# Conformer convolution: GpSimd's additions become accumulating DMAs into four partial sums, and the tap diagonals come from memory

## The chip, the cores and the metric

The program runs on one core of one Trainium2 chip. The metric is the device time of one execution in microseconds. Before the change it is 2589.65 us, the median of three runs (2588.46 to 2589.95).

## The reference, cut to what matters

The whole program is two transformer blocks of two layers each on a sequence of 512 tokens with 1024 features, in float32. The change lies in one of its mixers, the Conformer convolution of the second block, and in the padding of small tiles elsewhere.

```python
def conformer_conv(h, w_pw1, b_pw1, w_dw, b_dw, ln_g, ln_b, w_pw2, b_pw2):
    a, gt = jnp.split(h @ w_pw1 + b_pw1, 2, axis=-1)
    z = a * jax.nn.sigmoid(gt)
    z = lax.conv_general_dilated(
        z, w_dw[:, None, :], window_strides=(1,), padding=[(CONV_WIDTH - 1, 0)],
        dimension_numbers=('NWC', 'WIO', 'NWC'), feature_group_count=D_MODEL) + b_dw
    z = jax.nn.silu(layernorm(z, ln_g, ln_b))
    return z @ w_pw2 + b_pw2
```

So each of 1024 channels is convolved over time with its own 31 taps: y[t] is the sum over k of w[k] z[t - 30 + k].

## The kernel before, in words

Activations stand with 128 channels on the partitions and 512 tokens along the row; the 1024 channels are eight tiles, 0 to 7. Every matrix product in float32 is made of three TensorE matmuls (`mm3`, L325 to L327) on a high and a low half of each operand. `load` (L315, L307) brings a block of weights with one DMA of 512 KB issued by SyncE (SP) into `raw` (3 buffers), then ScalarE (ACT) casts it to `hi` and VectorE (DVE) subtracts to get `lo` (3 buffers each). In the trace, PE is TensorE, PEld its weight loads, POOL is GpSimd.

The Conformer stage (`conformer`, L1194) runs through the tiles in the order of `CONV_ON` (L193). For each tile the two halves of the first projection are made (`pw1`, two blocks of 24 matmuls), then `evict` (L1329) makes z with DVE and ACT, and `conv` (L1214) hands the tile's 31 taps out. The list says to whom: tiles 0, 2 and 5 wholly to DVE (`by_vector`, one multiply-and-add L1273 per tap, 90 in all beside the first tap, which is ACT's at L1231); tiles 1 and 3 wholly and 19 taps of tile 4 to ACT and POOL together (`by_pool`: ACT multiplies z by the tap, L1285, into `pr`, 4 buffers, and POOL adds `pr` to the sum `zc`, L1289, 79 times); 12 taps of tile 4 and all of tiles 6 and 7 to PE (`by_pe`, L1304: each tap is a product with a diagonal matrix, three matmuls into the bank `pcv`, 74 taps). The diagonals are made on the chip by `build` (L1296): ACT writes the high half `dh` (L1300), DVE the low half `dl` (L1301).

What is done beside what is set by the fillers `bg["v"]`, `bg["g"]`, `bg["p"]`, which hand out steps at a nominal price, and in the end by the scheduler, which lays down one fixed order for each engine. Each engine then works strictly in its order.

When three tiles are ready, `provisional` (L1255) sums them (L1258, L1259), PE makes their mean (`pm`), and every tile is shifted by it (`shift`, L1268), squared and summed (`centre`). After the last tile four columns of sums (`pd`, `pst`) give the layer norm, and the second projection (`pw2`) begins.

Of the kernel before, what the change touches and what calls it, by code (L numbers as in the profile page):

```python
# [2 lines left out]

# [1 line left out]

# [5 lines left out]
F32 = mybir.dt.float32  # L11
# [6 lines left out]
P = 128  # L18
# [41 lines left out]
def _lay_out(i):  # L60
# [98 lines left out]
    o["pw1"] = pairs(g["conv_w_pw1_2"][0], D)  # L159
    o["pw2"] = per_tile(g["conv_w_pw2_2"][0])  # L160

    q = np.arange(P)[:, None]
    c = np.arange(T)[None, :] - 384
    f = np.float32
# [26 lines left out]
PRIO_W = 100  # L191
CONV_V = .55
CONV_ON = [(0, "v", 0), (1, "g", 0), (2, "v", 0), (3, "g", 0), (4, "g", 12), (5, "v", 0), (6, "v", 31), (7, "v", 31)]  # L193
AHEAD = 12
NT_F = 2
NT_N = 2
GRP = 8
X_AT = (0, 1, 2)
ON_N = (1, 3)
ON_NV = (0,)  # L200
# [54 lines left out]
def _body(ctx, tc, a, out):  # L255
# [14 lines left out]

    def narrow(pool, n, dt=F32, **kw):

        return pool.tile([P, -(-n // 16) * 16], dt, **kw)[:, :n]

    nvec = a["vecs"].shape[1]
    vecs = narrow(cp, nvec, name="vecs")
# [221 lines left out]
    class Head:  # L498
# [4 lines left out]

        def scores(self):
            pool = self.pool
            nm = narrow(pool, NQ, name="nm", tag="nm", bufs=3)
            sm = narrow(pool, NQ, name="sm", tag="sm", bufs=3)
            self.p = []
            for i in range(NQ):
                n = P * (i + 1)  # L510
                acc = bank("sc")
                self.score(acc[:, :n], i, n)
                lg = pool.tile([P, n], F32, name=f"lg{i}", tag=f"lg{i}", bufs=2)
                V.tensor_tensor_reduce(out=lg, in0=acc[:, :n], in1=self.mask[:, T - n :], scale=-self.scale,  # L514
                                       scalar=3e38, op0=OP.add, op1=OP.min, accum_out=nm[:, i : i + 1])
                S.activation(lg, lg, AF.Exp, bias=nm[:, i : i + 1], scale=-1.0, accum_out=sm[:, i : i + 1])  # L516
                self.p.append(lg)
            rc = narrow(pool, NQ, name="rc", tag="rc", bufs=3)
            V.reciprocal(rc, sm)  # L519
            if self.rows_scale is not None:  # L520
                V.tensor_mul(rc, rc, self.rows_scale)
            for i in range(NQ):
                if i in self.on_s:
                    S.activation(self.p[i], self.p[i], AF.Copy, scale=rc[:, i : i + 1])
                else:
                    (V if i in self.on_v else G).tensor_scalar(self.p[i], self.p[i], rc[:, i : i + 1], None, op0=OP.mult)  # L526
# [373 lines left out]
    def nsa():  # L900
        with ExitStack() as es:
# [46 lines left out]
            with phase("n_x") as pool:  # L948
# [8 lines left out]
                def c_proj(m):  # L957
                    w = load(a["nsa_c"][m], NC8)
                    acc = bank()
                    yield from lin(acc, w, xs, range(NC8), sl(0))  # L960

                    def out():
                        bl = pool.tile([P, 16, 2, 32], F32, name="bl")
                        for g in range(2):
                            kst = pool.tile([P, T + 16], F32, name="kst", tag="kst")
# [112 lines left out]
            def u_task(gi):  # L1078
# [13 lines left out]
                hd = pool.tile([P, 16], F32, name="hd")  # L1092
# [20 lines left out]
            def cmp_scores(g):  # L1113
# [12 lines left out]
                mx = pool.tile([P, NQ * 4], F32, name="cmx", tag="cmx")  # L1126
# [3 lines left out]
                sm = pool.tile([P, NQ, 4], F32, name="csm", tag="csm")  # L1130
# [63 lines left out]
    def conformer():  # L1194
        with ExitStack() as es:
# [8 lines left out]

            with phase("c_x") as pool:

                nw = 31 * NC8
                wdw = vecs[:, _VECS["w_dw"][0] : _VECS["w_dw"][0] + nw]
                wdh = narrow(pool, nw, F32R, name="wdh")
                wdl = narrow(pool, nw, name="wdl")  # L1210
                S.copy(wdh, wdw)
                V.tensor_sub(wdl, wdw, bc(wdh))

                def conv(j, z, on, n_pe):  # L1214

                    y = zc[:, j]
                    if n_pe:
                        zh = narrow(pool, T + 30, F32R, name="zh", tag="zh", bufs=2)
                        zl = narrow(pool, T + 30, F32R, name="zl", tag="zl", bufs=2)
                        for t in (zh, zl):  # L1220
                            G.memset(bc(t[:, :30]), 0.0)
                        split(zh[:, 30:], zl[:, 30:], z)
                        bg["p"].push(j, by_pe(j, y, zh, zl, n_pe))
                    if n_pe < 31:
                        bg[on].push(j, (by_vector if on == "v" else by_pool)(j, y, z, n_pe))

                def start(j, y, z, n_pe):
                    if n_pe:
# [46 lines left out]
                        yield 660.0  # L1275
                    convolved(j)

                def by_pool(j, y, z, n_pe):
                    taps = list(start(j, y, z, n_pe))
                    prs = []  # L1280
                    for n in range(len(taps) + 3):
                        if n < len(taps):
                            sh = 30 - taps[n]
                            pr = pool.tile([P, T], F32, name="pr", tag="pr", bufs=4)
                            S.activation(pr[:, sh:], z[:, : T - sh], AF.Copy, scale=vec("w_dw", j * 31 + taps[n]))  # L1285
                            prs.append((pr, sh))
                        if n >= 3:
                            pr, sh = prs.pop(0)
                            G.tensor_add(y[:, sh:], y[:, sh:], pr[:, sh:])  # L1289
                        yield 1170.0  # L1290
                    convolved(j)

                taps = iter([j * 31 + k for j in order for k in range(plan[j][1])])
                diags = []

                def build(n):  # L1296
                    for t in islice(taps, n):
                        dh = pool.tile([P, P], F32R, name="dh", tag="dh", bufs=AHEAD + 2)
                        dl = pool.tile([P, P], F32R, name="dl", tag="dl", bufs=AHEAD + 2)
                        S.activation(dh, ident, AF.Copy, scale=vec("w_dw", t))  # L1300
                        V.tensor_scalar(dl, ident, wdl[:, t : t + 1], None, op0=OP.mult)  # L1301
                        diags.append((t, dh, dl))

                def by_pe(j, y, zh, zl, n_pe):  # L1304
                    acc = bank("pcv")
                    for k in range(n_pe):
                        build(1)
                        t, dh, dl = diags.pop(0)
                        assert t == j * 31 + k
                        mm3(acc, dh, dl, zh[:, k : k + T], zl[:, k : k + T], k == 0, k == n_pe - 1)  # L1310
                        yield STEP
                    if n_pe < 31 or not shifted:
                        S.activation(y, acc, AF.Identity, bias=vec("b_dw", j))
# [15 lines left out]
                def evict(j, acc, acg):  # L1329
                    sg = pool.tile([P, T], F32, name="sg", tag="sg", bufs=2)  # L1330
                    V.tensor_mul(sg, acg, norm.b)
                    at_s = S.activation(sg, sg, AF.Sigmoid, bias=vec("b_pw1", 8 + j))
                    z = pool.tile([P, T], F32, name="z", tag="z", bufs=8)
                    V.tensor_mul(z, acc, norm.b)  # L1334
                    at_v = V.scalar_tensor_tensor(z, z, vec("b_pw1", j), sg, op0=OP.add, op1=OP.mult)  # L1335
                    conv(j, z, *plan[j])
                    with tc.issue_after(at_s.ins), tc.issue_after(at_v.ins):
                        build(min(GRP, AHEAD - len(diags)))

                for j in order:  # L1340
                    accs = []
# [103 lines left out]
```

## Time and profile before

| | |
|---|---|
| median of three runs | 2589.65 us |
| the profiled execution, its own time | 2589.92 us |
| its span, first to last instruction | 2588.1 us |
| PE busy | 2512.7 us (97%) |
| DVE busy | 1626.9 us (63%) |
| ACT busy | 1141.1 us (44%) |
| POOL busy | 467.1 us (18%) |
| DMA queues, share of 16 engines' span | 26.6% |

The page cuts the span into 40 slices of 65 us. Read along PE's row of digits there is a 9 almost everywhere, and 7s and 8s in three or four slices from the thirty-first on: that is the Conformer stage. The granted clock of PE dips in the same slices. A stage is best read with the view that gives each engine's busy time by stretch, then the chain of waits in that stretch, then the groups of instructions by line.

### The profile page before, as it was taken

To read this page: it belongs to the slowest core of one execution; us is meant where nothing else is said; L and a number is where in the kernel's file an instruction comes from. 1 tells how busy PE (TensorE), PEld (TensorE's weight loads), DVE (VectorE), ACT (ScalarE), POOL (GpSimd) and SP (SyncE) were. 2 spreads that over 40 slices of the span, in tenths; PEclk is the share of its full clock that TensorE was granted. 3 is DMA by queue.
4 is the path that set the end of the run, shared out by engine and by line. 5 is a ranking of instruction groups with operands and counts; after the bars stand their busy time and mean duration, and the time that the engine had idled before them with its cause. 6 is when DMAs were issued, how large, how long until landed. Compare 5 with 4: busy or idle time off the path is not lost. (4 is left out here: it accounts for less than half of the span.)

```text
span 2588.1 us, 31317 instructions
## 1 busy us (share of the span) xinstructions
PE 2512.7 (97%) x11903; PEld 2088.8 (81%) x11903; DVE 1626.9 (63%) x2495; ACT 1141.1 (44%) x1933; POOL 467.1 (18%) x369
## 2 busy tenths in 40 slices
PE   8999999999999999999999999999999778999998
PEld 6988888888888888888888888888887556888886
DVE  7887777635677657777436996444338996544422
ACT  4664444424566544444334684322225453333221
POOL 3452000001132212000011222000004763100001
PEclk9999999999999999999999999999999878999998
DMA  4121333333211222332333212333332101323332
GB/s 151 59 67 66 106 98 98 92 96 104 90 55 56 72 73 90 99 97 93 93 97 114 65 54 82 98 98 96 90 100 74 57 17 33 99 97 98 94 98 70
DMA packets 65447, 218.90 MB, mean 85 GB/s; under 512 B 7536, under 2 KB 8560, under 8 KB 65296
## 3 DMA queue, kind: packets, MB, share of 16 engines
q1 hardware_dynamic: 65296, 216.90, 26.6%
q8 instruction: 93, 1.52, 0.2%
q14 instruction: 58, 0.48, 0.1%
HBM read 214.70 MB, written 2.10 MB: 84 GB/s over the span
## 5 line engine op out<-in xcount | busy, mean ns | idle before, releaser
L307 ACT CAST hi<-raw 128x1024 fp32r<-128x1024 f32 (+4 forms) x417 | 420.7, 1011 | 905.2 <-PE acc L326 707.0
L327 PE MATMUL acc<-xsh,lo 128*128 128x512 f32 x1792 | 701.1, 392 | 14.1 <-DVE lo L307 14.1
L325 PE MATMUL acc<-xsh,hi 128*128 128x512 f32 x1792 | 700.8, 392 | 3.0 <-ACT xsh L307 2.9
L326 PE MATMUL acc<-xsl,hi 128*128 128x512 f32 x1792 | 701.0, 391 | 1.0 <-DVE xsl L309 1.0
L307 DVE TENSOR_TENSOR lo<-raw,hi 128x1024 fp32r<-128x1024 f32 (+4 forms) x417 | 499.8, 1199 | 314.4 <-ACT hi L307 309.1
L327 PEld LDWEIGHTS acc<-xsh,lo 128*128 128x128 f32 x1792 | 338.7, 189 | 87.7 <-DVE lo L307 17.0
L325 PEld LDWEIGHTS acc<-xsh,hi 128*128 128x128 f32 x1792 | 338.8, 189 | 73.6 <-ACT xsh L307 3.3
L326 PEld LDWEIGHTS acc<-xsl,hi 128*128 128x128 f32 x1792 | 338.6, 189 | 73.2 <-DVE xsl L309 2.3
L377 POOL TENSOR_TENSOR ssum<-ssum,sq 128x512 f32<-128x512 f32 x75 | 120.8, 1614 | 1471.5 <-ACT sq L371 1461.4
L325 PE MATMUL acc<-hh,hi 128*128 128x512 f32 x704 | 277.4, 394 | 0.0
L327 PE MATMUL acc<-hh,lo 128*128 128x512 f32 x704 | 276.0, 392 | 0.0
L326 PE MATMUL acc<-hl,hi 128*128 128x512 f32 x704 | 273.2, 388 | 0.0
L526 POOL TENSOR_SCALAR lg<-lg,rc 128x384 f32<-128x384 f32 (+3 forms) x144 | 166.9, 1176 | 378.9 <-DVE rc L519 303.9
L714 DVE TENSOR_TENSOR y<-acc,r 128x512 f32<-128x512 f32 x88 | 60.5, 691 | 219.7 <-PE acc L327 219.5
L461 DVE TENSOR_TENSOR x<-x,acc 128x512 f32<-128x512 f32 x104 | 70.5, 684 | 153.5 <-PE acc L327 153.0
L327 PEld LDWEIGHTS acc<-hh,lo 128*128 128x128 f32 x704 | 132.1, 188 | 31.0
L326 PEld LDWEIGHTS acc<-hl,hi 128*128 128x128 f32 x704 | 132.2, 188 | 29.6
L325 PEld LDWEIGHTS acc<-hh,hi 128*128 128x128 f32 x704 | 132.3, 188 | 26.3
L1289 POOL TENSOR_TENSOR zc<-zc,pr 128x496 f32<-128x496 f32 (+17 forms) x79 | 127.7, 1620 | 64.5 <-ACT pr L1285 56.0
L711 DVE SCALAR_TENSOR_TENSOR y<-u,vecs,y 128x510 f32<-128x510 f32 (+1 forms) x176 | 130.9, 748 | 3.4 <-ACT y L709 0.6
L516 ACT ACTIVATE lg<-lg,nm 128x128 f32<-128x128 f32 x192 | 107.1, 560 | 47.4 <-DVE nm L514 46.4
L307 ACT CAST hh<-y 128x512 fp32r<-128x512 f32 x88 | 54.7, 621 | 135.5 <-DVE y L718 135.5
(366 smaller groups left out, 3841.4 us busy)
## 6 DMA issues: line engine op xcount, KB each, us to landing
raw<-in_ffn_in SPq DMA_DIRECT2D x88, 512.0 KB
raw<-in_swi_in SPq DMA_DIRECT2D x88, 512.0 KB
raw<-in_ffn_out SPq DMA_DIRECT2D x32, 448.0 KB
raw<-in_swi_out SPq DMA_DIRECT2D x32, 448.0 KB
raw<-in_pw SPq DMA_DIRECT2D x24, 512.0 KB
raw<-in_fox_qk SPq DMA_DIRECT2D x16, 512.0 KB
raw<-in_ffn_out SPq DMA_DIRECT2D x16, 512.0 KB
raw<-in_uqk SPq DMA_DIRECT2D x16, 512.0 KB
```

What stands on the lines that cost most here:

```text
L307: return S.copy(hi, src), V.tensor_sub(lo, src, bc(hi))
L325: PE.matmul(acc, lh, rh, start=first, stop=False)
L326: PE.matmul(acc, lh, rl, start=False, stop=False)
L327: last_mm[0] = PE.matmul(acc, ll, rh, start=False, stop=last).ins
L377: (sum_on or G).tensor_add(self.s, self.s, sq)
L461: V.tensor_add(x[:, c], x[:, c], acc)
L516: S.activation(lg, lg, AF.Exp, bias=nm[:, i : i + 1], scale=-1.0, accum_out=sm[:, i : i + 1])
L526: (V if i in self.on_v else G).tensor_scalar(self.p[i], self.p[i], rc[:, i : i + 1], None, op0=OP.mult)
L711: V.scalar_tensor_tensor(y[:, sh:], u[:, : T - sh], vec(f"cw{l}{2 - sh}", jj), y[:, sh:], op0=OP.mult, op1=OP.add)
L714: V.tensor_mul(y, acc, norm.b)
L1289: G.tensor_add(y[:, sh:], y[:, sh:], pr[:, sh:])
```

## The change

GpSimd's addition is replaced by a DMA that it issues and that accumulates (`accum_op=OP.add`): the DMA engines read `pr`, add it to the destination and write it. The sum of a tile is spread over four partial sums (`CHAINS = 4`): the sum `zc` itself and three tiles `part`, whose first taps ACT writes directly. After the last tap two DMAs add two of the partial sums to the other two, and a third joins those. So 70 DMAs carry products and 9 join partial sums, 79 in all, each of up to 128 x 2 KB (256 KB). `pr` has 8 buffers.

The diagonals are laid out beforehand on the host (`dwd`, 8 taps in a block of 128 x 1024) and come through `load`: 10 blocks, seven of 8 taps, two of 7 and one of 4. `build`, `wdh` and `wdl` go. Narrow tiles are padded to 128 bytes instead of 64, and three small tiles of a softmax head become slices of one.

```diff
+    wd = g["conv_w_dw_2"][0]
+    dg = np.zeros((sum(-(-n // 8) for _, _, n in CONV_ON), P, 8, P), np.float32)
...
+            dg[b + k // 8, np.arange(P), k % 8, np.arange(P)] = wd[k, j * P : (j + 1) * P]
...
+    o["dwd"] = dg.reshape(-1, P, RAW)
...
-AHEAD = 12
+CHAINS = 4
+STEP_G = 1000.0
...
-        return pool.tile([P, -(-n // 16) * 16], dt, **kw)[:, :n]
+        return pool.tile([P, -(-n // 32) * 32], dt, **kw)[:, :n]
...
-            nm = narrow(pool, NQ, name="nm", tag="nm", bufs=3)
-            sm = narrow(pool, NQ, name="sm", tag="sm", bufs=3)
+            small = narrow(pool, 3 * NQ, name="nm", tag="nm", bufs=3)
+            nm, sm, rc = (small[:, NQ * z : NQ * z + NQ] for z in range(3))
...
-                def by_pool(j, y, z, n_pe):
+                def by_dma(j, y, z, n_pe):
+
                     taps = list(start(j, y, z, n_pe))
-                    prs = []
...
-                            pr = pool.tile([P, T], F32, name="pr", tag="pr", bufs=4)
-                            S.activation(pr[:, sh:], z[:, : T - sh], AF.Copy, scale=vec("w_dw", j * 31 + taps[n]))
...
-                            G.tensor_add(y[:, sh:], y[:, sh:], pr[:, sh:])
-                        yield 1170.0
+                    parts = [y]
+                    for n, k in enumerate(reversed(taps)):
+                        sh = 30 - k
+                        if len(parts) < CHAINS:
+                            part = pool.tile([P, T], F32, name="part", tag="part", bufs=2 * (CHAINS - 1))
+                            if sh:
+                                G.memset(part[:, :sh], 0.0)
+                            S.activation(part[:, sh:], z[:, : T - sh], AF.Copy, scale=vec("w_dw", j * 31 + k))
+                            parts.append(part)
+                        else:
+                            pr = pool.tile([P, T], F32, name="pr", tag="pr", bufs=8)
+                            S.activation(pr[:, sh:], z[:, : T - sh], AF.Copy, scale=vec("w_dw", j * 31 + k))
+                            G.dma_start(parts[n % CHAINS][:, sh:], pr[:, sh:], accum_op=OP.add)
+                        yield STEP_G
+                    while len(parts) > 1:
+                        half = len(parts) // 2
+                        for to, of in zip(parts[:half], parts[half:]):
+                            G.dma_start(to, of, accum_op=OP.add)
+                        parts = parts[:half]
+                        yield STEP_G
                     convolved(j)
...
                     for k in range(n_pe):
-                        build(1)
-                        t, dh, dl = diags.pop(0)
-                        assert t == j * 31 + k
-                        mm3(acc, dh, dl, zh[:, k : k + T], zl[:, k : k + T], k == 0, k == n_pe - 1)
+                        if k % 8 == 0:
+                            n = min(8, n_pe - k)
+                            wh, wl = load(a["dwd"][first[j] + k // 8][:, : n * P], n)
+                        mm3(acc, wh[:, k % 8], wl[:, k % 8], zh[:, k : k + T], zl[:, k : k + T], k == 0, k == n_pe - 1)
```

Outside the Conformer stage the order and the waits of every engine stay as they were. Inside it they move at three places. Names in square brackets are what a row waits for: the engines by name, `DMAHW` a load of SP's, and `DMASW0` to `DMASW7` the landing of one of the eight latest DMAs that POOL issued.

On POOL, at the end of tile 1's taps. Before:

```order
L1289 TENSOR_TENSOR zc<-zc,pr 128x508 [waits Activation_49,Pool_49]
L1289 TENSOR_TENSOR zc<-zc,pr 128x509 [waits Activation_49,Pool_49]
L1289 TENSOR_TENSOR zc<-zc,pr 128x482 [waits Activation_49]
L1289 TENSOR_TENSOR zc<-zc,pr 128x510 [waits Activation_49,Pool_49]
L1289 TENSOR_TENSOR zc<-zc,pr 128x483 [waits Activation_49,Pool_49]
L1289 TENSOR_TENSOR zc<-zc,pr 128x511 [waits Activation_49,Pool_49]
```

After:

```order
L1293 DMA zc<-pr 128x507 [waits Activation_49]
L1293 DMA part<-pr 128x506 [waits Activation_49]
L1293 DMA part<-pr 128x505 [waits Activation_49]
L1298 DMA zc<-part 128x512 [waits DMASW7_49,DMASW1_49,Pool_49]
L1293 DMA part<-pr 128x504 [waits DMASW2_49,DMASW0_49,Activation_49]
L1298 DMA part<-part 128x512 [waits DMASW3_49,Pool_49]
L1293 DMA zc<-pr 128x503 [waits DMASW4_49,Activation_49]
L1293 DMA part<-pr 128x502 [waits DMASW5_49,Activation_49]
L1293 DMA part<-pr 128x501 [waits DMASW6_49,Activation_49]
L1293 DMA part<-pr 128x500 [waits DMASW0_49,Activation_49]
L1298 DMA zc<-part 128x512 [waits DMASW7_49,DMASW1_49]
```

Each addition waited for the one before it on POOL itself. Now each DMA waits for the landing of the DMA four places earlier, on the same partial sum, and the joins (L1298) stand in the same queue.

On DVE, where the first two finished tiles are summed. Before:

```order
L1273 SCALAR_TENSOR_TENSOR zc<-z,vecs,zc 128x496 [waits DVE_49]
L1334 TENSOR_TENSOR z<-acc,r 128x512 [waits PE_49]
L1258 TENSOR_TENSOR s_17771<-zc 128x512 [waits DVE_49,Pool_49]
L307 TENSOR_TENSOR lo<-raw,hi 128x1024 [waits DMAHW0_49,Activation_49]
L1273 SCALAR_TENSOR_TENSOR zc<-z,vecs,zc 128x497 [waits DVE_49]
```

After:

```order
L1273 SCALAR_TENSOR_TENSOR zc<-z,vecs,zc 128x499 [waits DVE_49]
L1258 TENSOR_TENSOR s_17517<-zc 128x512 [waits DMASW5_49,DMASW6_49,DMASW1_49,Pool_49]
L1273 SCALAR_TENSOR_TENSOR zc<-z,vecs,zc 128x484 [waits DVE_49]
L1273 SCALAR_TENSOR_TENSOR zc<-z,vecs,zc 128x500 [waits DVE_49]
L1334 TENSOR_TENSOR sg<-acc,r 128x512 [waits PE_49]
L1273 SCALAR_TENSOR_TENSOR zc<-z,vecs,zc 128x485 [waits DVE_49]
L315 TENSOR_TENSOR lo<-raw,hi 128x1024 [waits DMAHW1_49,Activation_49]
```

The sum over tiles 0 and 1 waited for POOL; now DVE's queue waits there for the landing of tile 1's joins, and the `lo` behind it is the first block of diagonals.

On ACT, at the last products of tile 4. Before:

```order
L1285 ACTIVATE pr<-z,vecs 128x501 [waits Pool_49]
L1300 ACTIVATE dh<-ident,vecs 128x128 [waits PE_49] x2
L1285 ACTIVATE pr<-z,vecs 128x502 [waits Pool_49]
L1300 ACTIVATE dh<-ident,vecs 128x128 [waits PE_49] x2
L1313 ACTIVATE zc<-pcv,vecs 128x512 [waits PE_49]
L1285 ACTIVATE pr<-z,vecs 128x503 [waits Pool_49]
```

After:

```order
L315 CAST hi<-raw 128x896 [waits DMAHW6_49,PE_49]
L1292 ACTIVATE pr<-z,vecs 128x497 [waits DMASW7_49,Activation_49]
L1292 ACTIVATE pr<-z,vecs 128x496 [waits DMASW0_49,Activation_49]
L1292 ACTIVATE pr<-z,vecs 128x495 [waits DMASW1_49]
L1292 ACTIVATE pr<-z,vecs 128x494 [waits DMASW2_49,Activation_49]
L315 CAST hi<-raw 128x1024 [waits DMAHW7_49,DVE_49,PE_49]
L315 CAST hi<-raw 128x1024 [waits DMAHW0_49,DVE_49,PE_49]
L315 CAST hi<-raw 128x1024 [waits DMAHW1_49,DVE_49,PE_49]
```

The single diagonals between the products are gone. Each product waits for the landing of the DMA that read its buffer last, and the casts of tile 7's diagonals (the three rows at the end) stand behind the last product of all.

## Rows read from the trace of the kernel before

**Rows 1.** Engines by stretch: busy us (instructions), PE's granted clock, DMA share, GB/s.

```profile
core 0: us, PE busy (x) PEld busy (x) DVE busy (x) ACT busy (x) POOL busy (x), PEclk, DMA share, GB/s
1900.00:1940.00 40.00, 40.00 (x177) 32.81 (x176) 11.84 (x14) 10.94 (x13) 4.38 (x3) 1.00 0.33 101
1980.00:2060.00 80.00, 65.92 (x252) 51.87 (x251) 79.97 (x65) 36.29 (x54) 60.88 (x38) 0.89 0.18 60
2060.00:2140.00 80.00, 57.27 (x182) 39.41 (x181) 79.96 (x108) 46.42 (x105) 55.08 (x38) 0.79 0.06 20
2140.00:2160.00 20.00, 10.81 (x46) 8.31 (x45) 16.07 (x29) 4.48 (x10) 5.58 (x5) 0.79 0.00 0
```

**Rows 2.** Chain of waits from 1957 to 2165 us, shares by engine and line.

```profile
by line: DVE zc L1273 41.6%; DVE dl L1301 17.4%; DVE lo L307 10.7%; issue 7.0%; DVE z L1335 4.4%; DVE zl L307 2.4%; DVE zc L1268 2.0%; DVE z L1334 1.9%; DVE d L1241 1.8%; DVE ssum L377 1.8%; PE acc L325 1.2%; DVE sg L1331 1.1%; PE pd L1365 
```

**Rows 3.** Groups by line, 1957 to 2155 us: busy us, mean ns, idle before, releaser.

```profile
L1289 POOL TENSOR_TENSOR zc<-zc,pr 128x496 f32<-128x496 f32 (+17 forms) x79 | 127.7, 1620 | 64.5 <-ACT pr L1285 56.0 <-DVE lo L307 4.5
L1273 DVE SCALAR_TENSOR_TENSOR zc<-z,vecs,zc 128x482 f32<-128x482 f32 (+21 forms) x90 | 99.4, 1122 | 0.2
L1285 ACT ACTIVATE pr<-z,vecs 128x494 f32<-128x494 f32 (+15 forms) x79 | 52.8, 699 | 1.7 <-POOL zc L1289 1.7
L1301 DVE TENSOR_SCALAR dl<-ident,wdl 128x128 fp32r<-128x128 f32 x74 | 42.1, 607 | 0.0
L327 PE MATMUL pcv<-zh,dl 128*128 128x512 f32 x74 | 35.3, 477 | 14.5 <-DVE dl L1301 14.2
L1300 ACT ACTIVATE dh<-ident,vecs 128x128 fp32r<-128x128 f32 x74 | 26.0, 390 | 8.8 <-PE pcv L326 8.6
L307 DVE TENSOR_TENSOR lo<-raw,hi 128x1024 fp32r<-128x1024 f32 x15 | 24.5, 1632 | 5.2 <-ACT hi L307 5.2
L1335 DVE SCALAR_TENSOR_TENSOR z<-z,vecs,sg 128x512 f32<-128x512 f32 x8 | 11.9, 1490 | 0.2 <-ACT sg L1332 0.2
```

**Rows 4.** Instructions in order of time on DVE and POOL: start us, us.

```profile
1964.76 2.23 DVE L1273 SCALAR_TENSOR_TENSOR zc<-z,vecs,zc 128x484 f32<-128x484 f32 x3
1968.26 1.22 DVE L307 TENSOR_TENSOR lo<-raw,hi 128x1024 fp32r<-128x1024 f32 x1
1972.30 17.19 POOL L1289 TENSOR_TENSOR zc<-zc,pr 128x482 f32<-128x482 f32 x10 [20.02 <-ACT pr L1285]
1982.83 2.26 DVE L307 TENSOR_TENSOR lo<-raw,hi 128x1024 fp32r<-128x1024 f32 x1
1988.30 5.09 DVE L1273 SCALAR_TENSOR_TENSOR zc<-z,vecs,zc 128x496 f32<-128x496 f32 x3
```

**Rows 5.** The stage's marks in order of time: first projection, products, last taps, second projection.

```profile
1943.59 0.40 PE L325 MATMUL acc<-xsh,hi 128*128 128x512 f32 x1
1971.53 2.46 ACT L1285 ACTIVATE pr<-z,vecs 128x482 f32<-128x482 f32 x4
2153.21 0.74 DVE L1317 SCALAR_TENSOR_TENSOR zc<-pcv,vecs,cmean 128x512 f32<-128x512 f32 x1
2154.73 1.87 PE L1365 MATMUL pd<-ones,d 128*128 128x1 f32 x8 [7.32 <-DVE d L1241]
2163.91 1.65 PE L325 MATMUL acc<-xsh,hi 128*128 128x512 f32 x3 [2.94 <-ACT xsh L307]
```

**Rows 6.** DMAs: a load's issue and its first reader, two stretches of full queues.

```profile
1.19 0.42 SPq L284 DMA_DIRECT2D x<-in_xt  x1
4.19 0.69 DVE L373 TENSOR_TENSOR ssum<-x 128x512 f32<-128x512 f32 x1 [4.19 <-DMA x<-in_xt]
...
8.00:10.00 2.00, 0.94 (x2) 0.03 (x1) 1.73 (x2) 1.09 (x2) 1.30 (x2) 1.00 1.04 412
2582.00:2584.00 2.00, 0.00 (x0) 0.00 (x0) 1.16 (x2) 0.00 (x0) 0.03 (x1) 0.50 1.02 382
```

More of the change, by code (lines that the diff above doesn't have):

```diff
@@ L1 @@
 from contextlib import ExitStack
-from itertools import islice
 import numpy as np
@@ L160, in _lay_out @@
     o["pw2"] = per_tile(g["conv_w_pw2_2"][0])
+    wd = g["conv_w_dw_2"][0]
+    dg = np.zeros((sum(-(-n // 8) for _, _, n in CONV_ON), P, 8, P), np.float32)
+    b = 0
+    for j, _, n in CONV_ON:
+        for k in range(n):
+            dg[b + k // 8, np.arange(P), k % 8, np.arange(P)] = wd[k, j * P : (j + 1) * P]
+        b += -(-n // 8)
+    o["dwd"] = dg.reshape(-1, P, RAW)
     q = np.arange(P)[:, None]
@@ L193 @@
 CONV_ON = [(0, "v", 0), (1, "g", 0), (2, "v", 0), (3, "g", 0), (4, "g", 12), (5, "v", 0), (6, "v", 31), (7, "v", 31)]
-AHEAD = 12
+CHAINS = 4
+STEP_G = 1000.0
 NT_F = 2
 NT_N = 2
-GRP = 8
 X_AT = (0, 1, 2)
@@ L517, in scores @@
                 self.p.append(lg)
-            rc = narrow(pool, NQ, name="rc", tag="rc", bufs=3)
             V.reciprocal(rc, sm)
@@ L964, in out @@
                         for g in range(2):
-                            kst = pool.tile([P, T + 16], F32, name="kst", tag="kst")
+                            kst = narrow(pool, T + 16, name="kst", tag="kst")
                             G.memset(kst[:, T - 1 :], 0.0)
@@ L1091, in u_task @@
                 wd = 2 << gi
-                hd = pool.tile([P, 16], F32, name="hd")
+                hd = narrow(pool, 16, name="hd")
                 V.tensor_mul(hd, cur[:, :16], cinv[:, sl(gi, 16)])
@@ L1125, in cmp_scores @@
                                            2.0 ** -(g * 4 + r + 1), a4[:, :, r], op0=OP.mult, op1=OP.add)
-                mx = pool.tile([P, NQ * 4], F32, name="cmx", tag="cmx")
+                mx = narrow(pool, NQ * 4, name="cmx", tag="cmx")
                 V.tensor_reduce(out=mx, in_=lg, axis=AX.X, op=OP.max)
@@ L1129, in cmp_scores @@
                 S.activation(lg, lg, AF.Exp)
-                sm = pool.tile([P, NQ, 4], F32, name="csm", tag="csm")
+                sm = narrow(pool, NQ * 4, name="csm", tag="csm").rearrange("p (i r) -> p i r", r=4)
                 V.tensor_reduce(out=sm.rearrange("p i r -> p (i r)"), in_=lg, axis=AX.X, op=OP.add)
@@ L1205, in conformer @@
             with phase("c_x") as pool:
[L1207 to L1212, printed above, removed]
                 def conv(j, z, on, n_pe):
@@ L1224, in conv @@
                     if n_pe < 31:
-                        bg[on].push(j, (by_vector if on == "v" else by_pool)(j, y, z, n_pe))
+                        bg[on].push(j, (by_vector if on == "v" else by_dma)(j, y, z, n_pe))
                 def start(j, y, z, n_pe):
@@ L1276, in by_vector @@
                     convolved(j)
-                def by_pool(j, y, z, n_pe):
+                def by_dma(j, y, z, n_pe):
                     taps = list(start(j, y, z, n_pe))
-                    prs = []
-                    for n in range(len(taps) + 3):
-                        if n < len(taps):
-                            sh = 30 - taps[n]
-                            pr = pool.tile([P, T], F32, name="pr", tag="pr", bufs=4)
-                            S.activation(pr[:, sh:], z[:, : T - sh], AF.Copy, scale=vec("w_dw", j * 31 + taps[n]))
-                            prs.append((pr, sh))
-                        if n >= 3:
-                            pr, sh = prs.pop(0)
-                            G.tensor_add(y[:, sh:], y[:, sh:], pr[:, sh:])
-                        yield 1170.0
-                    convolved(j)
@@ L1293, in conformer @@
[L1293 to L1302, printed above, removed]
+                    parts = [y]
@@ L1304, in by_pe @@
+                    while len(parts) > 1:
[4 more added lines that the diff above has]
+                        yield STEP_G
+                    convolved(j)
+                first = {}
+                for c, _, n in CONV_ON:
+                    first[c] = sum(-(-m // 8) for d, _, m in CONV_ON if d < c)
                 def by_pe(j, y, zh, zl, n_pe):
@@ L1331, in evict @@
                     V.tensor_mul(sg, acg, norm.b)
-                    at_s = S.activation(sg, sg, AF.Sigmoid, bias=vec("b_pw1", 8 + j))
+                    S.activation(sg, sg, AF.Sigmoid, bias=vec("b_pw1", 8 + j))
                     z = pool.tile([P, T], F32, name="z", tag="z", bufs=8)
                     V.tensor_mul(z, acc, norm.b)
-                    at_v = V.scalar_tensor_tensor(z, z, vec("b_pw1", j), sg, op0=OP.add, op1=OP.mult)
+                    V.scalar_tensor_tensor(z, z, vec("b_pw1", j), sg, op0=OP.add, op1=OP.mult)
                     conv(j, z, *plan[j])
-                    with tc.issue_after(at_s.ins), tc.issue_after(at_v.ins):
-                        build(min(GRP, AHEAD - len(diags)))
                 for j in order:
```

## The prediction

> **What bounds the kernel now.** I read the busy times by stretch first. For 40 us before the Conformer stage PE is busy all of the time at clock 1.00, 177 matmuls, 0.226 us each. Between 1980 and 2140 us DVE is busy 159.9 of 160 us, PE only 123.2, and PE's granted clock averages 0.89 and 0.79 of its 2.4 GHz, that is, part of the stretch at 1.2 GHz; the DMA engines are nearly idle (0.18 and 0.06) [rows 1]. So in this stage, and only here, DVE sets the pace. The chain of waits says the same: of 1957 to 2165 us, 41.6% is DVE's tap L1273 and 17.4% its low diagonals L1301, which PE waits for [rows 2, 3]. The next question is why DVE is so slow. The order of time shows it: three taps take 2.23 us before POOL starts its additions at 1972.30 and 5.09 us while POOL adds; a `lo` takes 1.22 and then 2.26 us [rows 4]. Both engines slow each other down; POOL's own additions take 1.62 us and leave it 64.5 us idle [rows 3].
>
> After the Trainium skill (SBUF — State Buffer, Who interferes with whom) a DVE instruction with two SBUF inputs contends with a GpSimd instruction that reads SBUF, not with one that only writes. The first half agrees with the two prices of a tap, 0.74 and 1.70 us; no row here shows a GpSimd that only writes descriptors.
>
> **The change part by part.** I count on the clock of the profiled execution (span 2588.1, own time 2589.92, 0.3 us above the median). Everything ahead of the stage keeps order and waits; the wider padding and the merged small tiles change no instruction's size, and I price them at nothing. The sum is the time at which the second projection starts, 2163.9 us before [rows 5].
>
> *DVE.* From 1957 to 2155 it is busy about 198 us without a gap. The 74 low diagonals go: -42.1. The 90 taps at 0.72 (mean of the eight ahead of 1972.30, as the 2.23 us for three also show) instead of 99.4 us: -34.6. The eight L1335 at 0.75 instead of 11.9 us: -5.9; three `zl` likewise: -2.9. The `lo` become 25 of 1.22 instead of 15 with 24.5 us: +6.0 [rows 3, 4]. Net -79.5: DVE's own work would end at 2075.5.
>
> *PE.* The first projection starts at 1943.59 [rows 5]; 384 matmuls of it and 222 of taps at 0.226 us are 137.0 us, small matmuls 2.5: it could be done at 2083.1. From the last eviction (2153.21) to the second projection it is 10.7 us [rows 5], work of the layer norm that the change does not touch. So PE's floor is 2093.8, a gain of 70.1 us.
>
> *ACT.* 79 products stay (52.8 us, nine of them written straight into partial sums); 74 high diagonals go (26.0), ten casts of about 1.0 come. ACT gets lighter by 16 us and is under half busy. But each product now waits for a landing, and casts that PE needs are behind products.
>
> *Loads.* Ten more on SP's queue, at most 5.2 MB, in a stretch where the DMA engines are used 0.06 to 0.18 [rows 1]: hidden as prefetch while three buffers are free; they share the engines with the additions, which I count below.
>
> *The additions.* 79 DMAs. The first product for one is ready at about 1974 (three products of the row at 1971.53 fill the partial sums) [rows 5]. Let T be the time from one DMA to the next. Nothing in the trace shows an accumulating DMA, or any issued by POOL, so I bound T. Full queues move 382 to 412 GB/s [rows 6]: 256 KB in 0.64 to 0.69 us. From below: an addition costs as much as a copy, 0.69, and 26 loads of 512 KB at about 1.31 us share the engines with 79 additions, 0.43 each: 1.1. If reading the destination counts as much again: 1.8. A load of 256 KB is read 3.0 us after its issue [rows 6]; if the four partial sums didn't overlap at all, T would be 3.0. I take 1.5, between the two ends that keep the four in flight; the full range is 1.1 to 3.0. POOL's own part in each issue is not shown either; SP's takes 0.42 [rows 6], POOL's old addition 1.62 [rows 3], so it doesn't move these ends.
>
> Three places turn T into a time. (a) Last landing: 1974 + 79 T, plus 12 for joins that nothing overlaps (one landing of 3.0 for each of the first two tiles, two for the last), plus about 11 (shift, square and sum 1.8, then 9.2 from `pd` at 2154.73 to 2163.91 [rows 5]): 1997 + 79 T. (b) The casts of tile 7's diagonals are behind the last product, which needs the landing of about the 66th DMA: 1974 + 66 T + 9, cast and `lo` 2, 93 matmuls 21, layer norm 10.7: 2017 + 66 T. (c) PE's floor, 2094. The latest counts. At T = 1.5 these are 2115.5, 2116 and 2094; the second projection starts at 2116 to 2117, 47 us earlier. On DVE the sum over tiles 0 and 1 (L1258) then waits for about the 39th landing, 1974 + 39 x 1.5 + 9 = 2041, where DVE would be at about 2020; behind it stand z of later tiles and the first block's `lo`. With 58 us of its work left it still ends by 2100, inside (a) and (b).
>
> Forecast: 2589.9 - 47 = 2543, to the median less 0.3: 2542. (What PE's higher clock gives back is in the sum, since the matmuls were priced at 0.226.)
>
> **The rivals.** *The DMAs are hidden* (T up to 1.2): PE's floor decides, 2589.9 - 70 = 2520. For it: 0.69 us of transfer and 1.1 with the loads. Against: three queues with hardly any slack, each waiting for landings.
>
> *An addition reads twice* (T = 1.8). Both operands are read by the DMA engines, so the transfer doubles to 1.38, with loads 1.8: (a) gives 2139, 25 us earlier, 2565. This is still faster. The Trainium skill (Collectives: The Full Stack, The bandwidth ceiling) puts the half rate of its ReduceScatter down to exactly that, two source reads per chunk on one ring; no run here shows it yet.
>
> *The DMA queue becomes the bound* (slower). Place: POOL's queue, where each DMA waits for the landing four places back, so T is at least a quarter of a landing, and ACT and DVE wait behind. It decides from T = 2.11, a landing of 8.4 us or 2.1 us of POOL's time per issue: 1997 + 79 x 2.11 = 2164. At T = 2.5: 2194.5, 31 us later, 2620; at 3.0: 2234, 2660. For it: every one of the 79 needs a round trip, the row shows 3.0 us for a plain load, and an addition has to read its destination first, on engines that also serve loads. Against: four are in flight, and 3.0 would have to grow nearly threefold.
>
> *DVE isn't relieved*: if POOL's issuing slows DVE as its additions do, the 43 us on taps and z come back in part: even all of them end DVE at 2119, the second projection at 2130, 2556. Faster still, since the diagonals are gone.
>
> **How the numbers follow.** Hidden 0.15; forecast band (T from 1.2 to 1.7, 2522 to 2557) 0.32; reads twice or DVE not relieved (2557 to 2584) 0.18; within 0.2%, 5 us, which is about what a measurement of this kernel can tell from no change (T about 2.05 to 2.17): 0.06; queue-bound 0.29, of which 0.13 lies beyond 2620. Faster 0.65, same 0.06, slower 0.29. The range 2518 to 2620 leaves that 0.13 out above and a little below PE's floor. The likeliest case alone spans 2522 to 2557.
>
> **What would show it.** In the profile after: taps L1273 at 0.72 us throughout; no DVE wait longer than the one at L1258; the spacing of POOL's DMAs, 1.5 us right, over 2.1 and the time is lost; the clock of PE near 1.00 until about 2031 us, where the first projection ends; the second projection at about 2117. I am wrong if ACT's products wait long on DMASW and casts with them, or if a tap still takes 1.7 us.

## The result and the profile after

The changed kernel takes 2576.85 us, median of four runs (2574.64 to 2577.25), against 2589.77 us for the kernel before (median with one more run of it); the ratio is 0.9949, interval 0.9932 to 0.9967. The forecast was 2542 us: of 47 us expected, 13 came. The profiled execution has a span of 2574.9 us.

The stretches of [rows 1], in the same columns, in the kernel after:

```profile
1900.00:1940.00 40.00, 40.00 (x173) 32.19 (x172) 11.86 (x13) 9.79 (x13) 2.84 (x2) 1.00 0.32 99
1980.00:2060.00 80.00, 70.73 (x291) 55.87 (x290) 56.34 (x77) 52.66 (x77) 39.76 (x47) 0.96 1.01 202
2060.00:2140.00 80.00, 56.49 (x217) 42.51 (x215) 52.82 (x75) 34.74 (x50) 29.98 (x36) 0.88 0.88 184
2140.00:2160.00 20.00, 16.19 (x60) 12.97 (x61) 15.11 (x25) 11.99 (x19) 9.40 (x7) 0.65 0.15 50
```

DVE, full before, is busy 109 of 160 us. Full is now another resource: the DMA share is 1.01 and 0.88, from 0.18 and 0.06. PE is hardly busier than before (127 of these 160 us, from 123). And one number ahead of the stage differs: 173 matmuls in 40 us at clock 1.00 instead of 177.

Groups by line, 1957 to 2155 us, as in [rows 3] (busy us, mean ns | idle before, releaser):

```profile
L1273 DVE SCALAR_TENSOR_TENSOR zc<-z,vecs,zc 128x482 f32<-128x482 f32 (+21 forms) x90 | 63.9, 731 | 9.0 <-ACT zc L1231 8.3
L1292 ACT ACTIVATE pr<-z,vecs 128x507 f32<-128x507 f32 (+27 forms) x70 | 48.2, 707 | 43.1 <-DMA part<-pr 33.6 <-DMA zc<-pr 9.3
L1293 POOL DMA_DIRECT2D part<-pr x52 | 47.6, 1004 | 58.0 <-ACT pr L1292 26.3 <-DMA part<-pr 23.4 <-issue 4.2
L315 DVE TENSOR_TENSOR lo<-raw,hi 128x1024 fp32r<-128x1024 f32 (+2 forms) x27 | 32.2, 1193 | 36.1 <-ACT hi L315 36.1
L333 PE MATMUL pcv<-zh,hi 128*128 128x512 f32 x74 | 31.2, 421 | 12.1 <-ACT hi L315 12.1
```

A tap of DVE costs 0.73 us, a `lo` 1.19 (1.12 and 1.63 before). What waits now, waits for DMAs: ACT's products 43 us for landings, and behind them DVE's `lo` 36 us and PE 12 us for ACT's casts.

The chain of waits, 1957 to 2155 us, by line, as in [rows 2]:

```profile
by line: DMA part<-pr 32.0%; DMA zc<-pr 16.8%; issue 7.1%; PE acc L333 5.8%; PE acc L334 5.5%; PE acc L335 5.1%; DMA part<-part 4.8%; DMA zc<-part 3.3%; ACT pr L1292 3.3%; POOL part L1293 3.0%; ACT hi L315 2.6%; DVE d L1241 1.4%; PE pst L39
```

The four kinds of additions hold 57% of it. The DMA queues between 1960 and 2150 us (packets, MB, share of 16 engines: q0 the additions, q1 the loads), and the first products' and the joins' issues (ns min/median/max, first and last start):

```profile
q0 software_dynamic: 11376, 20.16, 62.5%
q1 hardware_dynamic: 3806, 13.43, 21.3%
```

```profile
L1293 POOL DMA_DIRECT2D part<-pr x52: 860/869/2103, 1986.0 to 2106.9; - x52
L1298 POOL DMA_DIRECT2D zc<-part x6: 869/869/884, 2034.7 to 2127.0; - x6
```

79 DMAs from 1986.0 to 2127.0 are 78 spacings of 1.81 us: that is T. An addition takes 62.5% of 190 us / 79 = 1.50 us of all 16 engines. Marks in order of time (start us, us):

```profile
1955.19 0.39 PE L333 MATMUL acc<-xsh,hi 128*128 128x512 f32 x1
1985.96 1.08 POOL L1293 DMA_DIRECT2D part<-pr  x1 [22.12 <-ACT pr L1292]
2130.46 0.69 DVE L1268 TENSOR_TENSOR zc<-zc,cmean 128x512 f32<-128x512 f32 x1 [7.93 <-DMA zc<-part]
2149.48 1.65 PE L333 MATMUL acc<-xsh,hi 128*128 128x512 f32 x3 [2.91 <-ACT xsh L315]
```

The stage begins at 1955.2 instead of 1943.6 [rows 5]: 11.6 us are lost ahead of it, where nothing had been priced. The second projection begins 14.4 us earlier, not 47.

### The profile page after: what moved, and what is told of

It reads as the page before. It is cut to its first block, busy times and chain, and to the rows that moved or that the text cites. A ratio compares the mean times of both kernels' runs of the same rounds, so it can differ in the third digit from the quotient of the medians.

```text
span 2574.9 us, 31297 instructions
## 1 busy us (share of the span) xinstructions
PE 2512.4 (98%) x11903; PEld 2085.2 (81%) x11903; DVE 1550.0 (60%) x2430; ACT 1130.3 (44%) x1868; POOL 407.9 (16%) x377
## 5 line engine op out<-in xcount | busy, mean ns | idle before, releaser
L315 ACT CAST hi<-raw 128x1024 fp32r<-128x1024 f32 (+4 forms) x427 | 429.7, 1009 | 919.6 <-PE acc L334 723.2
L533 POOL TENSOR_SCALAR lg<-lg,nm 128x384 f32<-128x384 f32 (+3 forms) x144 | 165.9, 1167 | 383.0 <-DVE nm L526 314.8
L714 DVE TENSOR_TENSOR u<-acc,r 128x512 f32<-128x512 f32 x88 | 60.3, 687 | 73.9 <-PE acc L335 73.9
```

The source lines that it names most:

```text
L315: return S.copy(hi, src), V.tensor_sub(lo, src, bc(hi))
L714: V.tensor_mul(u, acc, norm.b)
```

## Experiments: what is lost ahead of the stage

Up to the stage order and waits are those of before; the matmuls of the second half of each feed-forward layer (`hh`, `hl`, 528 in a layer, four layers) start further apart (the pitch is the time from one start to the next). The first of them and the first of the next stage, before:

```profile
496.22 0.40 PE L325 MATMUL acc<-hh,hi 128*128 128x512 f32 x1
...
617.09 0.40 PE L325 MATMUL acc<-xsh,hi 128*128 128x512 f32 x1
```

and after:

```profile
496.94 0.40 PE L333 MATMUL acc<-hh,hi 128*128 128x512 f32 x1
...
620.14 0.39 PE L333 MATMUL acc<-xsh,hi 128*128 128x512 f32 x1
```

120.87 us became 123.20 us, without a gap and at the same clock. The suspect is the padding: it moves every tile behind the first narrow one.

**The padding put back**, alone, in the changed kernel:

```diff
-        return pool.tile([P, -(-n // 32) * 32], dt, **kw)[:, :n]
+        return pool.tile([P, -(-n // 16) * 16], dt, **kw)[:, :n]
```

> The changed kernel with one number put back: narrow tiles padded to 64 bytes as before, not 128. In the trace of after the matmuls that read hh and hl start 233.3 ns apart on average, before 228.9 ns; 2112 of them make 9 us, and the Conformer stage starts 11.6 us later. Theory (the padding moved the addresses, and these matmuls go slower at the new ones): pitch back at 229 ns, the first projection of the Conformer back at 1943 to 1944 us, time 2576.9 - 11.6 - 2.3 (the feed-forward layer behind the stage) = 2563. Rival (something else of the change slows them, say the new instructions or the merged small tiles): pitch stays at 233 ns, time 2575 to 2578.

Measured: 2563.83 us (2563.15 to 2565.44), ratio to before 0.9896 (0.9883 to 0.9910). The layer takes 120.87 us again, the Conformer begins at 1944.97. The merged small tiles are still in it, so they are not the cause. The theory holds.

**The padding and the merged tiles alone**, in the kernel before:

```diff
-        return pool.tile([P, -(-n // 16) * 16], dt, **kw)[:, :n]
+        return pool.tile([P, -(-n // 32) * 32], dt, **kw)[:, :n]
```

> The kernel before with only the wider padding and the merged small tiles. Theory of the addresses: pitch of the hh and hl matmuls 233 ns, Conformer's first projection at 1955, time 2589.8 + 14 = 2604. Rival (padding costs nothing, as predicted): 2590 within 2.

Measured: 2602.55 us (2602.36 to 2603.59), ratio 1.0045 (1.0033 to 1.0058). The layer takes 123.19 us. So the wider padding costs 12 us without the rest of the change and 13 us with it.

**What in the addresses.** Three kernels put an unused tile ahead of `hh`, of 432 numbers in a row (1728 bytes, shown), 352 (1408) or 176 (704):

```diff
+            pool.tile([P, 432], F32, name="gap")
             hs = hl(pool, HF, "h")
```

> The changed kernel at 64 bytes of padding, and in the feed-forward layers an unused tile of 1728 bytes ahead of hh, so that hh, hl and the weights hi, lo begin at the same place modulo 2048 bytes, as xsh and hi do, whose matmuls start 226.7 ns apart in both traces. Theory A (the distance between the two operands' addresses matters): pitch of hh and hl matmuls 226.7 instead of 229 ns, time 4 to 5 us below the run with 64 bytes alone, 2558 to 2559. Rival B (only each operand's own address matters, multiples of 128 being bad for one of them): no change or a rise, 2563 or more.

> The changed kernel itself, with its 128 bytes of padding, and an unused tile of 1408 bytes ahead of hh: hh and hl then begin at the same place modulo 2048 as hi and lo (640 bytes off in the changed kernel, 320 at 64 bytes). Theory A (the distance of the two operands modulo 2048 sets the pitch): pitch of hh and hl matmuls 226.7 ns instead of 233.3, time 2576.9 - 14 = 2563. Theory B (a tile at a multiple of 128 bytes is slow; here all of hh, hl, hi, lo are at multiples of 128): pitch stays at 233, time 2577.

> The changed kernel at 64 bytes with an unused tile of 704 bytes ahead of hh: the distance of hh to hi is 1024 modulo 2048, where 0 gave a pitch of 226.6 ns, 320 gave 228.9 and 640 gave 233.3. If the pitch grows with the distance, 236 to 240 ns, time 2563.8 + 15 to 23 = 2579 to 2587. If the distance counts modulo 1024 or 512, 226.6 ns and 2559 to 2561. If it is nearest to half of 2048 that counts less (1024 is no worse than 640): 229 to 233 ns.

| kernel | padding | start of `hh` less start of `hi` in the built program, modulo 2048 | first `hh` matmul to next stage, us | by 528, us |
|---|---|---|---|---|
| before | 64 | 320 | 120.87 | 0.2289 |
| changed, 64 | 64 | 320 | 120.87 | 0.2289 |
| changed | 128 | 640 | 123.20 | 0.2333 |
| before, 128 | 128 | 640 | 123.19 | 0.2333 |
| changed, 64, gap of 1728 | 64 | 0 | 119.68 | 0.2267 |
| changed, 64, gap of 704 | 64 | 1024 | 119.68 | 0.2267 |
| changed, gap of 1408 | 128 | 0 | 119.68 | 0.2267 |

The aligned one at 128 bytes, first `hh` matmul and the next stage's first:

```profile
497.27 0.39 PE L333 MATMUL acc<-hh,hi 128*128 128x512 f32 x1
...
616.95 0.39 PE L333 MATMUL acc<-xsh,hi 128*128 128x512 f32 x1
```

Times: 2561.06 us (2560.49 to 2561.77) for the gap of 1728, 2559.21 in one run for 704, 2562.37 (2560.68 to 2563.99) for 1408 at the wide padding. The first of them gave the pitch of theory A, but 2.8 us instead of the 4 to 5 that were expected. Theory A holds, B falls: in the last kernel all these tiles stand at multiples of 128 bytes, and its pitch is the shortest there is. The pitch doesn't grow with the distance either: 1024 costs nothing.

The pitches are means over 528 matmuls. In the trace's nanoseconds the starts of the aligned kernels follow each other at 226 or 227 throughout, those of the kernel before at 226, 229 and 232 in turn, those of the changed kernel at about 229 and 237. Block k of the weights begins 512 k bytes behind `hi`, while tile k of `hh` begins 2048 k bytes behind its start; so in an aligned kernel distances of 0 and 512 modulo 1024 take turns, and neither is dearer. The simplest reading is that the distance of the two operands counts modulo 256 or 512 bytes. It is not the only one: a distance of 0 was run at two places of `hh`, 320 and 640 at one each, so that the two places count each by itself is not excluded. What collides stays open too.

After the Trainium skill (SBUF — State Buffer, Who interferes with whom) PE's reads of the moving operand and its weight loads go through independent ports, and PE waits for nobody. The trace does not bear that out to the last per cent: the same matmuls on the same data start 0.2267, 0.2289 or 0.2333 us apart by the place of these two tiles. Whether one read waits for the other is not shown.

## Experiments: which half of the change brings the gain

All of these at 64 bytes.

**Diagonals from memory alone**; GpSimd still adds, by `by_pool` of before:

```diff
-                        bg[on].push(j, (by_vector if on == "v" else by_dma)(j, y, z, n_pe))
+                        bg[on].push(j, (by_vector if on == "v" else by_pool)(j, y, z, n_pe))
```

> One half of the change: diagonals from memory, additions still GpSimd's, padding 64 bytes. Theory (DVE is the bound, its taps still slowed by GpSimd's reads): low diagonals -42 us, ten more lo at 1.6 us +16, so second projection near 2138 and time 2564, taps still 1.1 us. Rival 1 (the accumulating DMAs bring the gain): 2580 or more. Rival 2 (GpSimd's additions become the bound, 79 at 1.62 us from 1972 with waits): second projection near 2150, 2576.

Measured: 2588.43 us (2587.32 to 2589.57), ratio 0.9989 (0.9980 to 0.9999). The theory falls, and the time is that of rival 1. DVE's groups, 1957 to 2155 us:

```profile
L1273 DVE SCALAR_TENSOR_TENSOR zc<-z,vecs,zc 128x482 f32<-128x482 f32 (+21 forms) x90 | 113.5, 1285 | 1.5 <-ACT zc L1231 0.9
L315 DVE TENSOR_TENSOR lo<-raw,hi 128x1024 fp32r<-128x1024 f32 (+2 forms) x25 | 40.6, 1624 | 5.2 <-ACT hi L315 5.2
L1241 DVE TENSOR_TENSOR d<-d,zc 128x512 f32<-128x512 f32 x7 | 6.9, 992 | 0.0
L385 DVE TENSOR_TENSOR ssum<-ssum,sq 128x512 f32<-128x512 f32 x7 | 6.9, 988 | 0.0
```

The low diagonals are gone, 42.1 us. Back came 16.1 for `lo` (40.6 less 24.5), 14.1 for dearer taps (113.5 less 99.4) and 4.2 for `d` and `ssum`. DVE is still busy 79.9 and 79.6 of 80 us: beside GpSimd's additions a tap got dearer, and a `lo` stayed as dear as it was (1.62 us).

**Accumulating DMAs alone**; the diagonals still made on the chip: the kernel before with `by_dma`.

```diff
-                        bg[on].push(j, (by_vector if on == "v" else by_pool)(j, y, z, n_pe))
+                        bg[on].push(j, (by_vector if on == "v" else by_dma)(j, y, z, n_pe))
```

> The other half of the change alone on the kernel before (64 bytes of padding): additions are accumulating DMAs, the diagonals are still made on the chip. Theory (the gain is GpSimd's silence: taps at 0.73 us and short z and zl take 43 us off DVE, and the DMAs keep a spacing of 1.7 to 1.8): DVE's own work ends near 2112, last landing 1974 + 79 x 1.75 + 12 = 2124, second projection near 2137, time 2560 to 2566, as good as the whole change at 64 bytes (2563.8). Rival (the diagonals from memory carry it): 2580 or more, because ACT's high diagonals and DVE's low ones stand behind products that wait for landings.

Measured: 2562.16 us (2561.31 to 2563.80), ratio 0.9891 (0.9875 to 0.9908). As good as the whole change at 64 bytes. DVE's taps and low diagonals, 1957 to 2150 us:

```profile
L1275 DVE SCALAR_TENSOR_TENSOR zc<-z,vecs,zc 128x498 f32<-128x498 f32 (+27 forms) x90 | 64.4, 731 | 1.4 <-ACT zc L1233 1.1
L1313 DVE TENSOR_SCALAR dl<-ident,wdl 128x128 fp32r<-128x128 f32 x74 | 18.0, 287 | 0.0
```

Taps take 731 ns, and a low diagonal 287 ns instead of 607: with GpSimd only issuing, the 74 cost DVE 18.0 us. The additions that move off GpSimd bring the whole gain; diagonals from memory bring nothing beside them, and 2.4 us alone.

## Experiments: what sets the spacing of the DMAs

The spacing is the time from the first DMA of GpSimd to the last, by the number of steps between them. These kernels have 64 bytes of padding too.

**Plain copies** in place of additions (the sums are left out):

```diff
-                            G.dma_start(parts[n % CHAINS][:, sh:], pr[:, sh:], accum_op=OP.add)
+                            G.dma_start(parts[n % CHAINS][:, sh:], pr[:, sh:])
...
-                            G.dma_start(to, of, accum_op=OP.add)
+                            G.dma_start(to, of)
```

> The changed kernel at 64 bytes of padding with the 79 DMAs as plain copies of the same 256 KB: nothing is added, so 28 or so taps of each of three tiles are left out of the result. At 64 bytes with additions the spacing is 1.80 us and the DMA engines are full (1.03 to 1.11 in six windows of 20 us), 118 us of all 16 engines for 79 DMAs, 1.50 each. Theory (an addition reads its destination as well, and that doubles its time on the engines): share per DMA falls to 0.7 to 0.8 us, spacing to 1.25 to 1.35 (GpSimd issues no faster than 1.22 to 1.25 in a run), stage 30 us or more shorter, time 2530 to 2540. Rival 1 (moving 256 KB inside SBUF costs 1.5 us by itself): spacing stays 1.8, time 2563. Rival 2 (GpSimd's issue or the round trip of four chains bounds it): spacing 1.6 or more at engines that are not full.

**Half the columns**, accumulated (the other half of the sums is left out):

```diff
-                            G.dma_start(parts[n % CHAINS][:, sh:], pr[:, sh:], accum_op=OP.add)
+                            G.dma_start(parts[n % CHAINS][:, T // 2 :], pr[:, T // 2 :], accum_op=OP.add)
...
-                            G.dma_start(to, of, accum_op=OP.add)
+                            G.dma_start(to[:, T // 2 :], of[:, T // 2 :], accum_op=OP.add)
```

> The changed kernel at 64 bytes with each of the 79 accumulating DMAs on the last 256 columns alone (128 KB; the taps' first 256 columns are left out of three tiles). Theory (bytes on the DMA engines set the spacing): 0.75 us of all engines per DMA, spacing falls to GpSimd's 1.25 to 1.35, time 2530 to 2540. Rival (a fixed price per DMA, its descriptors or its round trip): spacing 1.6 to 1.8, time above 2555.

Queue q0 between 1940 and 2150 us, with additions (64 bytes of padding):

```profile
q0 software_dynamic: 11376, 20.16, 56.4%
```

with copies:

```profile
q0 software_dynamic: 5200, 20.16, 25.4%
```

and with half the columns:

```profile
q0 software_dynamic: 11376, 10.36, 32.9%
```

By 210 us / 79 that is 1.50, 0.675 and 0.87 us of all engines per DMA. Spacing: 1.80, 1.22 and 1.31 us; one run each of 2523.67 and 2530.56 us. The theory holds in both: with less to do on the DMA engines the spacing falls, and an addition takes them 2.2 times as long as a copy of the same bytes. Copies came out below everything that was expected of them (0.7 to 0.8 us, 1.25 to 1.35, 2530 to 2540). Copies also had fewer and larger packets, 5200. But halving the bytes at the same number of packets took 42% off: on a straight line through the two, 0.24 of the 1.50 us (an estimate) would not go with the bytes, so packets are not the main price. With copies PE becomes the bound: the second projection starts at 2096.57, where the sum put PE's floor at 2093.8. Its chain, 1957 to 2100 us, holds almost nothing but matmuls:

```profile
by line: PE acc L333 18.9%; PE acc L334 18.6%; PE acc L335 18.5%; PE pcv L333 12.1%; PE pcv L335 12.1%; PE pcv L334 12.1%; PE pr L402 1.1%; ACT zc L1383 1.1%; DVE lo L315 0.9%; PE pst L390 0.7%; POOL lnt L396 0.7%; issue 0.6%; PE pm L1261 0
```

The Trainium skill (Collectives: The Full Stack, The bandwidth ceiling) puts ReduceScatter at half the rate of AllGather because its add needs two source reads. The trace of these DMAs agrees in size, 1.50 against 0.675 us; that the second read is the reason is argued, not shown.

**Eight partial sums:**

```diff
-CHAINS = 4
+CHAINS = 8
```

> The changed kernel at 64 bytes with eight partial sums instead of four; still 79 DMAs. At four, a DMA takes 7 to 10 us from issue to landing at a spacing of 1.80 us. Theory (the DMA engines are full: 1.50 us of all 16 per addition, 0.4 for the loads): spacing stays 1.75 to 1.85, landings get longer, time 2560 to 2567. Rival (four in flight are too few for a landing of 7 to 10 us, so the round trip sets the spacing at a quarter of it): spacing falls to 1.5 or less, time 2545 or less.

Measured, in one run: 2566.24 us, spacing 1.77, as the theory had it. The round trip is not the limit.

## Experiments: a better version

**Tile 4 to DVE**, 60 DMAs instead of 79:

```diff
-CONV_ON = [(0, "v", 0), (1, "g", 0), (2, "v", 0), (3, "g", 0), (4, "g", 12), (5, "v", 0), (6, "v", 31), (7, "v", 31)]
+CONV_ON = [(0, "v", 0), (1, "g", 0), (2, "v", 0), (3, "g", 0), (4, "v", 12), (5, "v", 0), (6, "v", 31), (7, "v", 31)]
```

> The changed kernel at 64 bytes with the 19 taps of tile 4 given to DVE instead of DMAs: 57 or 60 DMAs are left, DVE gets 19 taps at 0.73 us, 14 us. Theory (the DMA engines are the bound of the stage and DVE has 5 to 8 us of every 20 free): last landing 1976 + 60 x 1.8 + 12 = 2096, DVE's own work ends near 2090, PE's floor 2094: second projection at 2100 to 2110, time 2527 to 2537. Rival 1 (DVE becomes the bound, since the fillers give it tile 4 behind tile 5): second projection above 2125, time above 2550. Rival 2 (waits for landings inside ACT's and DVE's order, not the number of DMAs, set the end): 2563.

Measured: 2556.65 us (2555.12 to 2558.39), ratio 0.9869 (0.9855 to 0.9884). The last DMA is issued at 2084.2, as expected, but the second projection starts only at 2131.0: place and time are those of rival 1. The engines by stretch, columns as in [rows 1]:

```profile
1980.00:2060.00 80.00, 68.47 (x272) 53.35 (x270) 53.08 (x74) 47.67 (x69) 41.41 (x48) 0.94 1.09 219
2060.00:2120.00 60.00, 47.34 (x188) 36.99 (x188) 57.22 (x83) 18.75 (x25) 7.14 (x10) 0.89 0.57 141
```

DVE (the third of the engines) is idle 27 of the first 80 us and nearly full afterwards, 57 of 60: its `lo` waits 21.5 us for casts, which stand on ACT behind products that wait 34.3 us for landings.

**Products behind casts.** Each product is placed behind the cast of the block that PE works on, and a step gets a dearer nominal price, here 1500:

```diff
-                            S.activation(pr[:, sh:], z[:, : T - sh], AF.Copy, scale=vec("w_dw", j * 31 + k))
+                            with tc.issue_after(cast[0].ins):
+                                S.activation(pr[:, sh:], z[:, : T - sh], AF.Copy, scale=vec("w_dw", j * 31 + k))
```

> The changed kernel at 64 bytes with ACT's products set behind the cast of the weight block that PE works on, and 1500 instead of 1000 as the nominal price of a step, so that casts no longer stand behind a queue of products that wait for landings. Theory (the DMA engines are the bound, not ACT's order): PE's waits for casts shrink, but the spacing stays 1.75 to 1.85 and the last landing near 2122, time 2558 to 2566. Rival (the order on ACT sets the end): time 2550 or less.

Measured: 2567.71 us (2566.34 to 2569.09), 4 us slower than without, spacing 1.95; both lie above what the theory expected. With 79 DMAs the rival falls: PE gets its casts earlier and then waits 30.8 us ahead of the layer norm for the last sums.

With 60 DMAs, three kernels have this, tile 4 on DVE and the gap of 1728 bytes; `STEP_G` and `CONV_V` are 1800 and 0.55, 1800 and 0.8, 1400 and 0.55:

```diff
-STEP_G = 1000.0
+STEP_G = 1800.0
...
-CONV_V = .55
+CONV_V = .8
```

> Three edits on the changed kernel at 64 bytes: the unused 1728 bytes ahead of hh, tile 4's 19 taps on DVE (60 DMAs left), and products paced behind the casts at 1800. With tile 4 on DVE alone the last of 60 DMAs was issued at 2084, ACT's products waited 34 us for landings, DVE's lo 21.5 us for ACT's casts, and DVE was full from 2080 to 2120: its work came late. Theory (ACT's order holds DVE and PE back): waits of lo for casts under 8 us, second projection near 2110, time 2556.7 - 3 - 20 = 2530 to 2538. Rival (DVE's own work and the order of its taps set the end): time 2550 to 2556.

> As the run before, with the share by which DVE's taps are handed out raised from 0.55 to 0.8, so that they stand earlier in DVE's order. Theory (DVE's taps are late, since their price was set for the slow ones of 1.1 us): time 5 us or more below the run before. Rival (earlier taps push lo and z back, and PE waits): the same or slower.

> The version with tile 4 on DVE, aligned and paced, at 0.55 as in the first of the two, with a nominal price of 1400 instead of 1800 for a step. At 1800 GpSimd's DMAs had gaps of 4 to 12 us behind ACT's products, spacing 2.2 us, and the layer norm waited 12 to 23 us for the last landings. Theory (pacing too slow): spacing 1.9 to 2.0, last DMA at 2090 instead of 2102, time 2533 to 2540. Rival (casts again behind products): 2545 or more.

Measured: 2545.19 us (2544.52 to 2546.71), 2543.54 us (2542.95 to 2544.18; ratio to before 0.9819, 0.9804 to 0.9834) and 2552.49 us (2550.41 to 2553.36). The first landed between its theory (2530 to 2538) and its rival (2550 to 2556). The second is the best, 33 us below the changed kernel, but 1.7 us below the first instead of 5. The third did what was expected of the DMAs (spacing 1.98, last at 2089.7) and was 7 us slower than the first all the same: the theory on pacing falls. In the best one:

```profile
1980.00:2060.00 80.00, 78.13 (x340) 63.58 (x340) 75.01 (x107) 44.64 (x65) 32.43 (x40) 1.00 1.01 216
2060.00:2140.00 80.00, 55.52 (x215) 43.17 (x214) 51.36 (x77) 33.43 (x50) 25.06 (x25) 0.79 0.49 107
```

PE and DVE are nearly full for the first 80 us, and so are the DMA engines (1.01); the rest of the way to PE's floor lies in the tail, where the last DMA is issued at 2105.

## Why the prediction was right and wrong

- **DVE is the bound and GpSimd's additions slow it**: right. Taps were put at 0.72 us and took 0.731, `lo` at 1.22 and 1.19. The Trainium skill (SBUF — State Buffer, Who interferes with whom) excepts a GpSimd that only writes. Taps of 731 ns beside 79 issues agree with it, though no row shows what an issue reads or writes.
- **The low diagonals as a gain of 42.1 us**: wrong as a gain of its own. Alone it was worth 2.4 us (2588.43 against 2590.85 for the kernel before, run beside it); beside a GpSimd that no longer adds the diagonals cost 18.0 us, on an engine that is not the bound any more.
- **The padding and the merged tiles, "I price them at nothing"**: the first step that failed. That they "change no instruction's size" is true, but the addresses moved. Of the 11.6 us ahead of the stage 7.0 lie in three feed-forward layers (3 x 2.33) and 4.6 in other matmuls; 2.3 more come in the fourth layer, behind the stage. By the runs it is 13.0 us.
- **T = 1.5**: the second, a term mis-sized. The bounds were good: a copy was put at 0.69 and took 0.675, and "if reading the destination counts as much again: 1.8" is what came, 1.81. The middle of the two was chosen, and no row spoke for the middle. The 0.31 too little over 79 DMAs are 24 us.
- **The sum.** With T = 1.81, 1997 + 79 T = 2140, and 11.6 later 2151.6; measured 2149.5. From the 2542 forecast it is 24 + 11.6, less 2, and 2.3 in the last feed-forward layer: 2578, measured 2576.85. Without the padding the rival *an addition reads twice* gives 2139 and 2565; the run at 64 bytes shows 2138.9 and 2563.8. That it fits so closely is in part luck. In the changed kernel the two queues fill the DMA engines between 1986 and 2130 us:

```profile
q0 software_dynamic: 11376, 20.16, 82.5%
q1 hardware_dynamic: 2736, 9.57, 19.5%
```

Of these 144 us an addition has 1.50 and the loads 0.36 for each addition, where the rival had 1.38 and 0.43: the addition was dearer, and fewer loads fell into its time.

- **Four in flight**: right that they overlap. That T is at least a quarter of a landing did not set it; with eight partial sums the spacing was 1.77 against 1.80.
- **(b), casts behind the last products**: the waits came (12.1 us on PE, 36.1 on DVE's `lo`), but with 79 DMAs they don't set the end. With 60, products moved behind casts and paced at 1800 were worth some 9 us (11.5 less 2.8 for the alignment), paced at 1400 only 1.4 (4.2 less 2.8). The order and the pacing were not run apart, so which of them brings the 9 us is not shown.
- **L1258 as DVE's longest wait**: wrong. DVE came there late and waited 1.5 us; the longest was 7.9 us at L1268, for the last landings.
- **Clock of PE near 1.00 until 2031**: until 2020. Of the stretches of 20 us from there to 2140 those in which PE is busy 9.0 to 17.4 us show 0.83 to 0.91, and the one in which it is busy 19.65 shows 1.00.
- **The range** held the time; the likeliest case alone (2522 to 2557) did not.

## What to carry to other kernels

An edit that moves addresses is not free because it moves no instruction: set the large operands of matmuls at the same place modulo 1024 as their weights, and compare the count of matmuls in a quiet stretch. When an engine hands work to the DMA engines, their time is a sum like any other: here an accumulating DMA took 2.2 times a copy's. Test the halves of a change apart: one half carried all, and the other looked like 42 us on paper.

## What the runs showed of the hardware

- At full clock matmuls of 128x512 started 0.2267, 0.2289 or 0.2333 us apart on average, with their operands' tiles 0 or 1024, 320 and 640 bytes apart modulo 2048.
- An accumulating DMA of 256 KB inside SBUF took 1.50 us of all 16 DMA engines, a plain copy 0.675.
- Taking slow work off DVE left it as full as before (79.9 of 80 us) while GpSimd went on adding: the remaining work got dearer, 1122 to 1285 ns a tap.
